# A hybrid decoder layer on one core: decode values as the stationary operand, the merge weighted by VectorE, and the third pattern's query blocks two at a time

## The chip, the core and the metric

The kernel runs on one core of a Trainium2 chip. The metric is the device time of one execution in microseconds (us), lower is better. The engines work side by side, each in the order in which its instructions stand: TensorE (PE, its weight loads PEld), VectorE (DVE), ScalarE (ACT), GpSimd (POOL), and SyncE (SP), which issues nearly all transfers and so holds one ordered queue of DMA issues.

## The reference, cut to what matters

One layer for a prompt of 1024 positions and eight decode sequences of one token. A single projection gives q, k and v for three attention patterns (8 heads of 64, dilation 1, 4 and 16) and the inputs of a Mamba-2 branch. Each pattern gives an output and a softmax sum per position; the three are merged by those sums; the merged 512 columns and 1024 columns of the gated, normalised Mamba branch go through one output projection.

```python
for g, (window, dil) in enumerate(ATTN_PATTERNS):
    o, lse = dilated_window_prompt(q, k, v, dil)      # prompt; softmax over at most 129 keys
    outs.append(o); lses.append(lse)
attn = merge_patterns(outs, lses)                     # softmax over the three patterns, weighted sum
...
sc = jnp.einsum('bthd,btkhd->bthk', q, sel_k) * ATTN_SCALE          # decode: 128 cached keys and the new one
o = jnp.einsum('bthk,btkhd->bthd', softmax(sc), sel_v)
...
mix = jnp.concatenate([attn, ssm], axis=-1) @ w_out
```

## The kernel before, in words

All activations lie transposed, 128 features by 1032 positions (1024 of the prompt and 8 decode tokens), eight such tiles for 1024 features. A projection of 128 output columns is called a gemm here: three chunks of 344 positions, each of 24 matmuls (L176: eight k tiles, three products of a high and a low part). Its weights are loaded to `wr` (L149), rounded to `wh` by ScalarE (L164), and the rest `wl` is made by VectorE (L165); the second matmul of a chunk needs `wl`.

The code is written in stages, but the order on each engine is set when the program is built, by a list scheduler with priorities ("evac", "w", "side", "late", "main") and its own estimates of time; small work is thus put between the matmuls of long gemms. At run time each engine keeps that order and waits on semaphores.

The stage that the change touches runs from about 780 to 1040 us. In it stand, one inside the other:

- **Pattern 2** (`attend`, L633): for each of four head pairs and eight blocks of 128 queries, score matmuls (L649), VectorE adds the mask and takes the maximum in one instruction with an accumulator (L655) and scales it (L659), ScalarE takes the exponential with a sum (L663), PE transposes (L670), a copy (L674 or L676), PE multiplies with the values (L683). The result goes to DRAM (`n_d`).
- **The z gemms** 0 to 7, 72 matmuls each; VectorE multiplies each into `yg[k]` (L886).
- **The merge** (L818 to L862, priority "late"): from the softmax sums the weights `wo` are made on VectorE (L844), transposed on PE (L845), stored to `w_d` and loaded back spread over partitions as `wt`. Then 16 merges, one for each 256 positions and head pair: load `nt` (three patterns, 384 KB) and `wt`, multiply (L858, GpSimd), two adds (L859, L860, VectorE), round to `ah` (L861, ScalarE), `al` = rest (L862, VectorE). `nt` and `wt` have two buffers each, so the load of merge k+2 waits for L862 of merge k.
- **Decode values** (L895 to L925): 24 loads `cvt` (eight sequences, three patterns, 128 cached rows of 512) on six buffers, 24 multiplies by the probabilities `dpt` (16 on GpSimd, 8 on VectorE), 16 adds on VectorE (L910, L911), eight matmuls with a selecting column (L912), four transposes.
- **The SSM output projection**: after the last z gemm ScalarE and VectorE make `sh` and `sl` of `yg` (L935, L936), and the first two column blocks are multiplied (L957), k tile by k tile; the rest are gemms again.

Of the kernel before, what the change touches and what calls it, by code (L numbers as in the profile page):

```python
# [50 lines left out]
def trunk(tc, a, o):  # L51
# [581 lines left out]
    def attend(g, hp, qr, kr, vt):  # L633
# [58 lines left out]
                                   nps.rearrange("p (r i) -> p r i", i=S // d))  # L692
        nc.sync.dma_start(out=n_d[g, hp], in_=nh)

    def pattern(g):
        for hp in range(HP):
            vt = do_v(g, hp)
            qr = do_qk(g, hp, 0)
            kr = do_qk(g, hp, 1)
            with prio("side"):  # L700
                attend(g, hp, qr, kr, vt)
        with prio("side"):
            stt = ac.tile([P, 8, 16], F32, name=f"stt{g}")
# [114 lines left out]
    with prio("late"):  # L818
# [30 lines left out]
        for q in range(S // QT):  # L849
            for hp in range(HP):  # L850
                qs = slice(q * QT, (q + 1) * QT)
                nt = mgp.tile([P, NG, QT], F32, tag="nt", name="nt")
                nc.sync.dma_start(out=nt, in_=n_d[:, hp, :, qs].rearrange("g p t -> p g t"))
                wt = mgp.tile([P, NG, QT], F32, tag="wt", name="wt")
                for h in range(2):
                    nc.sync.dma_start(out=wt[h * 64:(h + 1) * 64],
                                      in_=w_d[:, 2 * hp + h, qs].unsqueeze(0).to_broadcast([64, NG, QT]))
                nc.gpsimd.tensor_tensor(out=nt, in0=nt, in1=wt, op=ALU.mult)  # L858
                nc.vector.tensor_tensor(out=nt[:, 0], in0=nt[:, 0], in1=nt[:, 1], op=ALU.add)  # L859
                nc.vector.tensor_tensor(out=nt[:, 0], in0=nt[:, 0], in1=nt[:, 2], op=ALU.add)  # L860
                nc.scalar.copy(ah[:, hp, qs], nt[:, 0])  # L861
                nc.vector.tensor_tensor(out=al[:, hp, qs], in0=nt[:, 0], in1=ah[:, hp, qs], op=ALU.subtract)  # L862
# [30 lines left out]
                    nc.gpsimd.tensor_tensor(out=acc, in0=acc, in1=zt, op=ALU.add)  # L893

    with prio("late"):  # L895
        sel = cap.tile([P, NB * NB], F32, name="sel")
        nc.vector.memset(sel, 0.0)
        nc.vector.memset(sel[:, 0:NB * NB:NB + 1], 1.0)
        ops = att_ps("nps")
        for b in range(NB):  # L900
            vts = []
            for g in range(NG):
                vt = cvp.tile([P, 512], F32, tag="cv", name="cvt")
                nc.sync.dma_start(out=vt, in_=a[f"cache{g}"][b].rearrange("(k r) c -> r k c", r=DIL[g])[0, :, 512:1024])
                pw = dpt[:, g].rearrange("p h (x b) -> p b x h", b=NB)[:, b].unsqueeze(3)
                v4 = vt.rearrange("p (x h d) -> p x h d", x=HP, h=2)
                (nc.gpsimd if g else nc.vector).tensor_tensor(out=v4, in0=v4, in1=pw.to_broadcast([P, HP, 2, 64]),
                                                              op=ALU.mult)
                vts.append(vt)
            nc.vector.tensor_tensor(out=vts[0], in0=vts[0], in1=vts[1], op=ALU.add)  # L910
            nc.vector.tensor_tensor(out=vts[0], in0=vts[0], in1=vts[2], op=ALU.add)  # L911
            behind(nc.tensor.matmul(ops[:NB], sel[:, b * NB:(b + 1) * NB], vts[0], start=(b == 0), stop=(b == NB - 1)),  # L912
                   zlast[CACHE[b]])
        osb = cvp.tile([NB, 512], F32, tag="cv", name="osb")
        nc.scalar.copy(osb, ops[:NB])
        otp = att_ps("nps")
        for hp in range(HP):
            nc.tensor.transpose(otp[:, hp * NB:(hp + 1) * NB], osb[:, hp * P:(hp + 1) * P], ident[:NB, :NB])
        nc.vector.tensor_tensor(out=dat, in0=otp[:, 0:HP * NB], in1=dnv[:, 0], op=ALU.add)
        for g in range(1, NG):  # L920
            nc.vector.tensor_tensor(out=dat, in0=dat, in1=dnv[:, g], op=ALU.add)
        dv = dat.rearrange("p (h b) -> p h b", h=HP)
        nc.scalar.copy(ah[:, :, S:T], dv)
        nc.vector.tensor_tensor(out=al[:, :, S:T], in0=dv, in1=ah[:, :, S:T], op=ALU.subtract)
# [582 lines left out]
```

## Time and profile before

| what | value |
|---|---|
| time, median of 3 runs | 1864.06 us (1863.29 to 1867.74) |
| the profiled execution | 1859.84 us, its span 1858.1 us |
| PE busy in the span | 1773.7 us (95%) |
| VectorE, ScalarE, GpSimd busy | 1143.8, 782.1, 320.4 us |
| mean granted clock of TensorE | 0.982 |

PE is the bound nearly everywhere, so what counts is the time in which it waits or runs at half clock. A timeline row gives start, duration, engine, line, operation, tiles, and in brackets how long the engine had been idle and what ended that. A busy PE row is a model of a pipelined matmul; the distance between two starts tells more than the duration.

### The profile page before, as it was taken

What the parts mean: (1) busy time and instruction counts of PE and PEld (TensorE: products, weight loads), DVE (VectorE), ACT (ScalarE), POOL (GpSimd) and SP (SyncE); (2) the same over time, 40 slices, a digit from 0 to 9 for tenths busy, and PEclk for the clock granted to TensorE, in tenths of its full rate; (3) what the DMA queues carried; (4) which work ended last, traced back from release to release, by engine and by line L of the source; (5) the groups of instructions that cost most, each with busy time, mean ns of one, the idle gap of its engine ahead of it and who ended that gap; (6) DMA issues with size and microseconds to landing.
All of it is one profiled execution on the core that took longest, in us unless ns stands there. A gap on an engine that the chain in (4) does not pass through costs nothing.

```text
span 1858.1 us, 30703 instructions
## 1 busy us (share of the span) xinstructions
PE 1773.7 (95%) x12189; PEld 1659.7 (89%) x12189; DVE 1143.8 (62%) x2236; ACT 782.1 (42%) x1441; POOL 320.4 (17%) x217
## 2 busy tenths in 40 slices
PE   8999999999998999999879999999999999999995
PEld 6999877888887888988768999999999999999995
DVE  6545666776765454446577599886666666423338
ACT  5533554465544555556343335532222222431133
POOL 0000244544224221123342300000000000000020
PEclk9999999999999999999989999999999999999998
DMA  4322344434334243346566345364454445876686
GB/s 156 136 99 79 96 127 124 130 121 125 105 103 156 90 141 108 117 158 230 154 172 187 108 155 178 111 211 166 172 175 159 177 152 204 335 276 205 207 316 206
DMA packets 135200, 298.61 MB, mean 161 GB/s; under 512 B 18432, under 2 KB 85600, under 8 KB 133648
## 3 DMA queue, kind: packets, MB, share of 16 engines
q1 hardware_dynamic: 135056, 296.64, 48.2%
q8 instruction: 96, 1.57, 0.4%
q14 instruction: 48, 0.39, 0.1%
HBM read 247.49 MB, written 137.10 MB: 207 GB/s over the span
## 4 chain that ended last, share of the span: by engine, by line
PE 37%; DVE 8%; DMA 4%; issue 1%; ACT 1%; POOL 0%; SPq 0%; DVEq 0%; POOLq 0%; ACTq 0%
PE fb L1230 21%; PE g L176 15%; DMA nt<-n_d 2%; PE pg L176 1%; PE pu L176 1%; DVE wl L165 1%; DVE xr L1056 1%; DVE sl L936 1%; DVE nacc L1013 1%; DMA hr<-hid_d 0%; DMA cvt<-in_cache 0%; DVE nt L859 0%; POOL nt L858 0%; DMA wr<-in_w_fin 0%; DVE fl L1071 0%
## 5 line engine op out<-in xcount | busy, mean ns | idle before, releaser
L176 PE MATMUL g<-xh,wh 128*128 128x344 f32 x1344 | 445.0, 331 | 4.4 <-ACT rw L589 3.7
L176 PE MATMUL g<-xh,wl 128*128 128x344 f32 x1344 | 438.9, 327 | 7.2 <-DVE wl L165 7.2
L176 PE MATMUL g<-xl,wh 128*128 128x344 f32 x1344 | 440.6, 328 | 1.5 <-DVE xl L234 1.5
L176 PEld LDWEIGHTS g<-xh,wh 128*128 128x128 f32 x1344 | 256.5, 191 | 17.8 <-issue 8.4
L176 PEld LDWEIGHTS g<-xh,wl 128*128 128x128 f32 x1344 | 257.0, 191 | 15.0 <-DVE wl L165 8.0
L176 PEld LDWEIGHTS g<-xl,wh 128*128 128x128 f32 x1344 | 256.9, 191 | 7.8 <-issue 4.9
L1230 PE MATMUL fb<-fh,wsl 128*128 128x258 f32 x1216 | 222.3, 282 | 0.0
L1230 PEld LDWEIGHTS fb<-fh,wsl 128*128 128x128 f32 x1216 | 187.9, 189 | 0.0
L1230 PE MATMUL fb<-fl,wsl 128*128 128x258 f32 x608 | 171.7, 283 | 0.0
L165 DVE TENSOR_TENSOR wl<-wr,wh 128x1024 fp32r<-128x1024 f32 (+1 forms) x93 | 113.6, 1222 | 82.5 <-ACT wh L164 82.3
L176 PE MATMUL g<-hh,wh 128*128 128x344 f32 x432 | 137.9, 319 | 0.8 <-ACT fac L1297 0.8
L176 PE MATMUL g<-hh,wl 128*128 128x344 f32 x432 | 137.7, 319 | 0.0
L176 PE MATMUL g<-hl,wh 128*128 128x344 f32 x432 | 136.7, 320 | 0.0
L164 ACT CAST wh<-wr 128x1024 fp32r<-128x1024 f32 (+1 forms) x93 | 92.4, 995 | 93.5 <-PE g L176 87.8
L663 ACT ACTIVATE sm<-sm,ngm 128x128 f32<-128x128 f32 (+1 forms) x192 | 84.8, 443 | 108.9 <-DVE ngm L659 103.9
L1313 POOL TENSOR_TENSOR ow<-wr,ow 128x512 fp32r<-128x512 f32 x8 | 10.9, 1395 | 659.6 <-ACT ow L1312 659.6
L619 POOL TENSOR_TENSOR sw<-sw,sin 128x1032 f32<-128x1032 f32 x24 | 73.4, 3059 | 250.6 <-ACT sw L618 187.1
L1230 PEld LDWEIGHTS fb<-fl,wsl 128*128 128x128 f32 x608 | 114.8, 189 | 0.0
L618 ACT COPY sw<-rw 32x1032 f32<-32x1032 f32 x96 | 101.0, 1052 | 1.4
L589 ACT COPY rw<-g 128x344 f32<-128x344 f32 x108 | 47.2, 442 | 112.1 <-PE g L176 70.4
L1234 DVE TENSOR_TENSOR fo<-fp,fb 128x258 f32<-128x258 f32 x152 | 62.8, 420 | 46.1 <-PE fb L1230 43.7
L176 PEld LDWEIGHTS g<-hh,wh 128*128 128x128 f32 x432 | 81.1, 188 | 1.1 <-ACT fac L1297 1.1
(362 smaller groups left out, 3789.8 us busy)
## 6 DMA issues: line engine op xcount, KB each, us to landing
out_skv<-in_cache SPq DMA_DIRECT2D x64, 1023.5 KB, 5.8
wr<-in_w_in SPq DMA_DIRECT2D x56, 512.0 KB, 3.7
out_skv<-in_cache SPq DMA_DIRECT2D x16, 1022.0 KB, 5.5
wr<-in_w_out SPq DMA_DIRECT2D x24, 512.0 KB, 3.7
hr<-hid_d SPq DMA_DIRECT2D x22, 516.0 KB, 6.2
hid_d<-fo SPq DMA_DIRECT2D x38, 258.0 KB, 4.2
wg<-in_w_fin SPq DMA_DIRECT2D x19, 512.0 KB, 4.6
wu<-in_w_fin SPq DMA_DIRECT2D x19, 512.0 KB, 5.0
```

The costliest lines, as they stand in the source:

```text
L164: nc.scalar.copy(wh[:, :cols], wr[:, :cols])
L165: nc.vector.tensor_tensor(out=wl[:, :cols], in0=wr[:, :cols], in1=wh[:, :cols], op=ALU.subtract)
L176: last = nc.tensor.matmul(ps, x[:, ws], y[:, c0:c1], start=(k == 0 and j == 0), stop=(k == n - 1 and j == 2))
L589: return nc.scalar.copy(rw[:, c0:c1], ps)
L618: nc.scalar.copy(sw[q * 32:(q + 1) * 32, 0:T], rw[s * 32:(s + 1) * 32, :])
L619: nc.gpsimd.tensor_tensor(out=sw[:, 0:T], in0=sw[:, 0:T], in1=sin, op=ALU.mult)
L663: nc.scalar.activation(out=sm[:, h, :nk], in_=sm[:, h, :nk], func=AF.Exp, scale=SCALE, bias=ngm[:, g, j, i:i + 1], accum_out=den[:, g, j, ...
L936: nc.vector.scalar_tensor_tensor(out=lo, in0=yg[k][:, cs_], scalar=nw(SSD_NORM, k), in1=hi, op0=ALU.mult, op1=ALU.subtract)
L1013: nc.vector.tensor_tensor(out=acc, in0=acc, in1=sq, op=ALU.add)
L1056: nc.vector.scalar_tensor_tensor(out=h, in0=mv, scalar=nw(MIX_POST, m), in1=h, op0=ALU.mult, op1=ALU.add)
L1230: nc.tensor.matmul(ps, x[:, ks], y, start=(k == 0 and j == 0), stop=(k == 3 and j == 2))
L1234: return nc.vector.tensor_tensor(out=dst, in0=x, in1=y, op=ALU.add)
```

## The change

Three edits. (1) Pattern 2 goes through a new function `attend2`: two query blocks at a time, the mask added by two 128x256 instructions, one maximum, one subtraction and one sum over 128x512 on VectorE, one exponential of 128x512 on ScalarE. The matmuls are the same in number, in bursts of four. (2) The merge multiply goes from GpSimd to VectorE. (3) The decode values become the stationary operand: 96 products (each two instructions in the trace, as the float32 matmuls of before are) of a 128x128 block of `cvt` with the two probability columns of its heads replace the multiplies, the adds, the selecting matmuls and the transposes; the `cvt` buffers are freed by PE. No pool is changed.

```diff
+    def attend2(hp, qr, kr, vt):
...
+        for j in range(0, 8, 2):
+            sps = [att_ps("sps") for _ in range(2)]
...
+            for h in range(2):
+                nc.vector.tensor_tensor(out=sm[:, h], in0=sps[h][:, 0:2 * P].rearrange("p (i k) -> p i k", i=2),
+                                        in1=mask2.unsqueeze(1).to_broadcast([P, 2, P]), op=ALU.add)
+            i2 = slice(hp * 2, hp * 2 + 2)
+            mv = mx[:, g, j:j + 2, i2].rearrange("p i h -> p h i")
+            nc.vector.tensor_reduce(out=mv, in_=sm, op=ALU.max, axis=AX.X)
+            nc.vector.tensor_tensor(out=sm, in0=sm, in1=mv.unsqueeze(3).to_broadcast([P, 2, 2, P]), op=ALU.subtract)
+            nc.scalar.activation(out=sm, in_=sm, func=AF.Exp, scale=SCALE)
+            nc.vector.tensor_reduce(out=den[:, g, j:j + 2, i2].rearrange("p i h -> p h i"), in_=sm, op=ALU.add,
+                                    axis=AX.X)
+            tp = att_ps("ptp")
+            for h in range(2):
+                for i in range(2):
+                    q = h * 2 + i
+                    nc.tensor.transpose(tp[:, q * P:(q + 1) * P], sm[:, h, i], ident)
...
-                nc.gpsimd.tensor_tensor(out=nt, in0=nt, in1=wt, op=ALU.mult)
+                nc.vector.tensor_tensor(out=nt, in0=nt, in1=wt, op=ALU.mult)
...
-                pw = dpt[:, g].rearrange("p h (x b) -> p b x h", b=NB)[:, b].unsqueeze(3)
-                v4 = vt.rearrange("p (x h d) -> p x h d", x=HP, h=2)
-                (nc.gpsimd if g else nc.vector).tensor_tensor(out=v4, in0=v4, in1=pw.to_broadcast([P, HP, 2, 64]),
-                                                              op=ALU.mult)
                 vts.append(vt)
-            nc.vector.tensor_tensor(out=vts[0], in0=vts[0], in1=vts[1], op=ALU.add)
-            nc.vector.tensor_tensor(out=vts[0], in0=vts[0], in1=vts[2], op=ALU.add)
-            behind(nc.tensor.matmul(ops[:NB], sel[:, b * NB:(b + 1) * NB], vts[0], start=(b == 0), stop=(b == NB - 1)),
-                   zlast[CACHE[b]])
...
+            for x in range(HP):
+                q = x * NB + b
+                for g in range(NG):
+                    ins = nc.tensor.matmul(ops[:, 0:64].rearrange("p (h c) -> p h c", h=2)[:, :, q],
+                                           vts[g][:, x * P:(x + 1) * P], dpt[:, g, :, q], start=(g == 0),
+                                           stop=(g == NG - 1))
+                    if x == 0 and g == 0:
+                        behind(ins, zlast[CACHE[b]])
```

The scheduler then puts everything in another order. On VectorE before, the end of the z gemms reads as follows (L859, L860 and L862 belong to a merge, whose multiply is on GpSimd; L936 makes `sl` for the first SSM matmuls; six merges stand ahead of this first `sl`, the seventh between the first and the second):

```order
L886 TENSOR_TENSOR yg_9266<-yg_9266,zt 128x1032
L860 TENSOR_TENSOR nt<-nt 128x256
L859 TENSOR_TENSOR nt<-nt 128x256
L860 TENSOR_TENSOR nt<-nt 128x256
L862 TENSOR_TENSOR al<-nt,ah 128x256 x2
L936 SCALAR_TENSOR_TENSOR sl_9476<-yg_8721,par,sh_9475 128x688
L936 SCALAR_TENSOR_TENSOR sl_9476<-yg_8721,par,sh_9475 128x344
L859 TENSOR_TENSOR nt<-nt 128x256
L936 SCALAR_TENSOR_TENSOR sl_9478<-yg_8811,par,sh_9477 128x688
L936 SCALAR_TENSOR_TENSOR sl_9478<-yg_8811,par,sh_9477 128x344
L860 TENSOR_TENSOR nt<-nt 128x256
L936 SCALAR_TENSOR_TENSOR sl_9480<-yg_8902,par,sh_9479 128x688
```

After the change (L909 is the merge multiply, L910, L911 and L913 are L859, L860 and L862 of before, L982 is L936) the same place reads:

```order
L910 TENSOR_TENSOR nt<-nt 128x256
L911 TENSOR_TENSOR nt<-nt 128x256
L982 SCALAR_TENSOR_TENSOR sl_9387<-yg_8593,par,sh_9386 128x688
L982 SCALAR_TENSOR_TENSOR sl_9387<-yg_8593,par,sh_9386 128x344
L982 SCALAR_TENSOR_TENSOR sl_9389<-yg_8683,par,sh_9388 128x688
L982 SCALAR_TENSOR_TENSOR sl_9389<-yg_8683,par,sh_9388 128x344
L909 TENSOR_TENSOR nt<-nt,wt 128x768
L913 TENSOR_TENSOR al<-nt,ah 128x256
L982 SCALAR_TENSOR_TENSOR sl_9391<-yg_8774,par,sh_9390 128x688
L982 SCALAR_TENSOR_TENSOR sl_9391<-yg_8774,par,sh_9390 128x344
L910 TENSOR_TENSOR nt<-nt 128x256
L165 TENSOR_TENSOR wl<-wr,wh 128x1024
```

The merge multiplies are now on this engine, and fifteen of the sixteen merges stand ahead of the first `sl`. The weights' rest `wl` for the second SSM block (L165) stands behind the sixteenth.

On SP's queue before, around the store of the merge weights (L848), the loads of `nt` (L853), `wt` (L856), `cvt` (L904) and weights (L149) stand so:

```order
L853 DMA nt<-n_d 128x3x256 x2
L904 DMA cvt<-in_cache 128x512 x2
L848 DMA w_d<-wts 64x3x128
L856 DMA wt<-w_d 64x3x256 x4
L904 DMA cvt<-in_cache 128x512 x2
L856 DMA wt<-w_d 64x3x256 x2
L904 DMA cvt<-in_cache 128x512
L856 DMA wt<-w_d 64x3x256 x2
L904 DMA cvt<-in_cache 128x512
L149 DMA wr<-in_w_out 128x1024
L853 DMA nt<-n_d 128x3x256
L904 DMA cvt<-in_cache 128x512 x2
```

After (L899 is L848, L904 is the load of `nt`, L907 of `wt`, L952 of `cvt`):

```order
L904 DMA nt<-n_d 128x3x256 x2
L149 DMA wr<-in_w_in 128x1024
L899 DMA w_d<-wts 64x3x128
L907 DMA wt<-w_d 64x3x256 x4
L952 DMA cvt<-in_cache 128x512
L907 DMA wt<-w_d 64x3x256 x4
L904 DMA nt<-n_d 128x3x256
L952 DMA cvt<-in_cache 128x512
L904 DMA nt<-n_d 128x3x256
L952 DMA cvt<-in_cache 128x512 x4
L907 DMA wt<-w_d 64x3x256 x3
L904 DMA nt<-n_d 128x3x256
```

The `cvt` loads of the rest of the third and of the fourth sequence (three for each) now stand behind the loads of the third and fourth `nt`, which wait for the first two merges. On PE, the transposes of the merge weights stand 25 L176 matmuls earlier than before (after 3803 from the start, not 3828), the 96 products of decode values stand in bursts of 24, 24, 12, 12, 12 and 12 between the z gemms, and 229 L176 matmuls lie between those transposes and the first SSM matmul. Pattern 2's work, 57 bursts between the matmuls of the gemms before, stands in 34.

## Rows read from the trace of the kernel before

**Rows 1.** The page: busy us, share of the span, instructions of each engine.

```profile
PE 1773.7 (95%) x12189; PEld 1659.7 (89%) x12189; DVE 1143.8 (62%) x2236; ACT 782.1 (42%) x1441; POOL 320.4 (17%) x217
```

**Rows 2.** Waits of PE, 894 to 1045 us: engine, line, releaser, us, times, longest.

```profile
PE g L176 <- DVE wl L165: 11.5, 6, 4.1
...
PE g L957 <- DVE sl L936: 5.2, 1, 5.2
```

**Rows 3.** Timeline of PE: start, us, operation, [idle before it, what ended that].

```profile
899.79 0.66 PE L176 MATMUL g<-xh,wl 128*128 128x344 f32 x1 [4.09 <-DVE wl L165]
...
900.53 0.49 PE L176 MATMUL g<-xh,wh 128*128 128x344 f32 x1
...
905.70 0.36 PE L176 MATMUL g<-xh,wh 128*128 128x344 f32 x1
...
929.42 0.47 PE L176 MATMUL g<-xh,wl 128*128 128x344 f32 x1 [2.58 <-DVE wl L165]
```

**Rows 4.** Timeline of VectorE, 895 to 900 us.

```profile
897.91 0.69 DVE L911 TENSOR_TENSOR cvt<-cvt 128x512 f32<-128x512 f32 x1 [2.02 <-POOL cvt L907]
...
898.52 1.22 DVE L165 TENSOR_TENSOR wl<-wr,wh 128x1024 fp32r<-128x1024 f32 x1
```

**Rows 5.** Timeline of VectorE, 921 to 975 us.

```profile
924.17 1.99 DVE L860 TENSOR_TENSOR nt<-nt 128x256 f32<-128x256 f32 x1
...
960.22 0.42 DVE L859 TENSOR_TENSOR nt<-nt 128x256 f32<-128x256 f32 x1 [2.57 <-POOL nt L858]
...
962.75 1.42 DVE L936 SCALAR_TENSOR_TENSOR sl<-yg,par,sh 128x688 fp32r<-128x688 f32 x2 [0.69 <-ACT sh L935]
```

**Rows 6.** Timeline of PE at the first SSM matmuls.

```profile
971.04 0.65 PE L957 MATMUL g<-sl,wh 128*128 128x344 f32 x1 [5.25 <-DVE sl L936]
```

**Rows 7.** Timeline of PE around one attention burst.

```profile
879.68 0.32 PE L176 MATMUL g<-xh,wh 128*128 128x344 f32 x1
...
879.93 0.44 PE L683 MATMUL nps<-pt,vt 128*64 128x128 f32 x4
...
880.73 0.32 PE L176 MATMUL g<-xl,wh 128*128 128x344 f32 x1
...
880.89 0.32 PE L176 MATMUL g<-xh,wh 128*128 128x344 f32 x1
```

**Rows 8.** Groups by line and shape: count, busy us, mean ns, idle before.

```profile
L165 DVE TENSOR_TENSOR wl<-wr,wh 128x768 fp32r<-128x768 f32 x24 | 23.0, 957 | 29.8 <-ACT wh L164 29.8
...
L474 DVE TENSOR_REDUCE yd<-tm 128x4 f32<-128x512 f32 x16 | 11.0, 685 | 20.1 <-POOL tm L473 20.1
...
L663 ACT ACTIVATE sm<-sm,ngm 128x256 f32<-128x256 f32 x88 | 43.9, 500 | 48.4 <-DVE ngm L659 48.1
```

**Rows 9.** Timeline of PE, 905 to 913 us.

```profile
911.98 0.38 PE L845 MATMUL wtp<-ident,wo 128*64 128x128 f32 x2
```

**Rows 10.** Timeline of GpSimd, 905 to 990 us.

```profile
921.86 1.82 POOL L858 TENSOR_TENSOR nt<-nt,wt 128x768 f32<-128x768 f32 x1 [10.63 <-DMA wt<-w_d]
...
936.89 2.28 POOL L858 TENSOR_TENSOR nt<-nt,wt 128x768 f32<-128x768 f32 x1
...
981.62 1.98 POOL L858 TENSOR_TENSOR nt<-nt,wt 128x768 f32<-128x768 f32 x1 [11.77 <-DMA nt<-n_d]
```

**Rows 11.** DMA issues, 900 to 1030 us: count, KB each, median us to landing.

```profile
nt<-n_d SPq DMA_DIRECT2D x16, 384.0 KB, 4.9
```

**Rows 12.** Timeline of the DMA queue of SP, 912 to 985 us.

```profile
929.82 0.38 SPq L853 DMA_DIRECT2D nt<-n_d  x1
...
977.88 2.13 SPq L853 DMA_DIRECT2D nt<-n_d  x2
```

**Rows 13.** Windows: us, busy (instructions) of five engines, granted clock, DMA share, GB/s.

```profile
930.00:940.00 10.00, 10.00 (x51) 8.93 (x51) 8.73 (x8) 4.17 (x6) 6.51 (x4) 0.85 0.90 280
```

**Rows 14.** Timeline of PE: eight small matmuls; four of 128 columns.

```profile
198.41 0.66 PE L440 MATMUL dtp<-ident,dex 8*128 8x8 f32 x8
...
242.01 0.66 PE L670 MATMUL ptp<-ident,sm 128*128 128x128 f32 x4
```

More of the change, by code (lines that the diff above doesn't have):

```diff
@@ L693, in attend @@
         nc.sync.dma_start(out=n_d[g, hp], in_=nh)
+    def attend2(hp, qr, kr, vt):
+        g = 2
+        nh = nhp.tile([P, S], F32, tag="nh", name="nh")
+        for j in range(0, 8, 2):
+            sps = [att_ps("sps") for _ in range(2)]
+            for jj in (j, j + 1):
+                for h in range(2):
+                    hs = slice(h * 64, (h + 1) * 64)
+                    c0 = (jj % 2) * P
+                    js = slice(jj * P, (jj + 1) * P)
+                    nc.tensor.matmul(sps[h][:, c0:c0 + P], qr[hs, js], kr[hs, js], start=True, stop=True)
+            sm = smp.tile([P, 2, 2, P], F32, tag="sm", name="sm")
+            for h in range(2):
[9 more added lines that the diff above has]
+            tp = att_ps("ptp")
+            for h in range(2):
+                for i in range(2):
+                    q = h * 2 + i
+                    nc.tensor.transpose(tp[:, q * P:(q + 1) * P], sm[:, h, i], ident)
+            pt = ptp.tile([P, 4, P], F32, tag="pt", name="pt")
+            dst = pt.rearrange("p q t -> p (q t)")
+            if j % 4:
+                nc.scalar.copy(dst, tp)
+            else:
+                nc.vector.tensor_copy(dst, tp)
+            if j % 4 == 0:
+                nps = att_ps("nps")
+            for i in range(2):
+                for h in range(2):
+                    hs = slice(h * 64, (h + 1) * 64)
+                    nc.tensor.matmul(nps[hs, (j % 4 + i) * P:(j % 4 + i + 1) * P], vt[:, j + i, hs], pt[:, h * 2 + i],
+                                     start=True, stop=True)
+            if j % 4 == 2:
+                d = DIL[g]
+                rr = slice((j - 2) * d // 8, (j + 2) * d // 8)
+                nc.scalar.copy(nh.rearrange("p (i r) -> p r i", r=d)[:, rr],
+                               nps.rearrange("p (r i) -> p r i", i=S // d))
+        nc.sync.dma_start(out=n_d[g, hp], in_=nh)
@@ L700, in pattern @@
             with prio("side"):
-                attend(g, hp, qr, kr, vt)
+                if g == 2:
+                    attend2(hp, qr, kr, vt)
+                else:
+                    attend(g, hp, qr, kr, vt)
         with prio("side"):
@@ L895, in trunk @@
     with prio("late"):
-        sel = cap.tile([P, NB * NB], F32, name="sel")
-        nc.vector.memset(sel, 0.0)
-        nc.vector.memset(sel[:, 0:NB * NB:NB + 1], 1.0)
         ops = att_ps("nps")
@@ L904, in trunk @@
                 nc.sync.dma_start(out=vt, in_=a[f"cache{g}"][b].rearrange("(k r) c -> r k c", r=DIL[g])[0, :, 512:1024])
-                pw = dpt[:, g].rearrange("p h (x b) -> p b x h", b=NB)[:, b].unsqueeze(3)
-                v4 = vt.rearrange("p (x h d) -> p x h d", x=HP, h=2)
-                (nc.gpsimd if g else nc.vector).tensor_tensor(out=v4, in0=v4, in1=pw.to_broadcast([P, HP, 2, 64]),
-                                                              op=ALU.mult)
                 vts.append(vt)
-            nc.vector.tensor_tensor(out=vts[0], in0=vts[0], in1=vts[1], op=ALU.add)
-            nc.vector.tensor_tensor(out=vts[0], in0=vts[0], in1=vts[2], op=ALU.add)
-            behind(nc.tensor.matmul(ops[:NB], sel[:, b * NB:(b + 1) * NB], vts[0], start=(b == 0), stop=(b == NB - 1)),
-                   zlast[CACHE[b]])
[L914 to L919, printed above, removed]
+            for x in range(HP):
[6 more added lines that the diff above has]
+                        behind(ins, zlast[CACHE[b]])
+        for h in range(2):
+            hs = slice(h * 64, (h + 1) * 64)
+            nc.vector.tensor_tensor(out=dat[hs], in0=ops[hs, h * 32:(h + 1) * 32], in1=dnv[hs, 0], op=ALU.add)
         for g in range(1, NG):
```

## The prediction

> **What bounds the kernel now.** I read the page first: PE is busy in 1773.7 of 1858.1 us [rows 1], so an edit elsewhere counts only where PE waits or is slowed. The waits of PE in 894 to 1045 us, the stretch with the end of pattern 2, the merge and the decode values, come next [rows 2]: 11.5 us in six waits for `wl` and 5.2 us in one for `sl`, both made by VectorE. The timeline says what lies ahead of them. The longest, 4.09 us, ends at 899.79 [rows 3]; VectorE made that `wl` at 898.52, behind L911, which had waited for a multiply of decode values on GpSimd [rows 4]. After such a stall PE is also slow: from 900.53 to 905.70 [rows 3] eighteen matmuls start 0.29 us apart, where 0.16 us is the pace elsewhere (880.73 to 880.89 [rows 7]), so it ran at the lower of its two clock levels, 1.2 GHz, after the idle time. The last one, 5.25 us at 971.04 [rows 6], waits for the second `sl`, which stands behind the seventh merge. So the merge chain paces this stretch, and it is paced by itself: two buffers, and a load of `nt` that must wait for L862 two merges before.
>
> **Terms, edit by edit.** *Decode values.* The multiplies on GpSimd that held up `wl` are gone: the stall of 4.1 us at 899.79 goes, and with it the slow matmuls, 18 and three ahead of them, 0.13 us each, 2.7 us. In their place PE gets 96 products, 192 instructions. The trace has no such product. Bounds: eight small matmuls take 0.66 us, 0.083 us for one; four of 128 columns also take 0.66, 0.165 us for one [rows 14]. So 15.8 to 31.7 us; they move only two columns, so I take the lower value, 16 us. The Trainium skill (TensorE: Matmul & The Clock Gate, section LDWEIGHTS) would have a load of 128 columns take 107 ns, for which I estimate 20.5 us for 192; rows 14 show less for one small matmul, and no row shows 192 in a line. None of this is on the path if PE waits for the merge chain anyway, which the next sums decide.
>
> *Pattern 2.* A burst between two gemm matmuls costs about 0.09 us at its start: 879.68 to 879.93 is 0.25 us where 0.16 is the pace [rows 7]; I take the same at its end. Twenty-three bursts fewer (57 to 34), 0.18 us each, save 4.1 us. The softmax of one step becomes longer: two mask adds of 0.42 (960.22 has the size [rows 5]), a maximum and a subtraction of 0.69, an exponential that I put at 0.71 (0.50 us for 256 columns [rows 8], and twice that as an upper end). With hand-offs of 0.5 us that is 3.4 us from scores to transposes; the nearest stand 27 gemm matmuls apart, 4.2 us. It is covered, by 0.8 us. Uncovered it would cost up to 0.8 us in each of 16 steps.
>
> *The merge.* Its start comes earlier. The transposes of the weights end PE's part at 911.98 [rows 9]. From that go 4.1 and 2.7 (the stall and its slow matmuls), 4.1 (pattern 2) and 25 matmuls by which they stand earlier, 3.9 us: 897.2. The first multiply started 9.9 us behind them (921.86 [rows 10]), so 907.1 now. Of each merge, the multiply falls from 1.82 us or more [rows 10] to 0.96 (the 128x768 subtraction of VectorE [rows 8]); the two adds are 0.42 each when GpSimd is quiet (960.22), where one of them took 1.99 us at 924.17 while GpSimd multiplied [rows 5]. That contention goes away with the multiplies. The Trainium skill (SBUF — State Buffer, section SBUF: two separate sides) calls the port pair of the two engines an exclusive lock; by that rule the adds come back to 0.42, and the trace agrees.
>
> But 15 merges now stand ahead of the first `sl`, where six did. From one L862 to that of the merge two later: landing of `nt`, 4.9 us as the median [rows 11], then 0.96, two adds of 0.42, `ah` with hand-offs 0.53 and `al` 0.42, 2.75 in all; the other buffer's merge runs in the time of the landing. A leg is 7.65 us. The first L862 ends about 4 us behind the first multiply; then come seven legs, 53.6 us, and in three of them a `wl` and a `yg`, both near 1.22 us (898.52 is a `wl` [rows 4]), 7.3 us. The first `sl` starts at 907.1 + 4.0 + 53.6 + 7.3 = 972.0. It takes 0.92 us of the 1.42 of the two [rows 5], and PE then has six matmuls, 1.4 us at a pace between the two, up to the point that it reached at 971.04. That is 974.3, **3.3 us later**.
>
> Is PE there in time? From the transposes it has 229 gemm matmuls, 36 us, 16 us of products, and waits for `cvt` and `wl`. The `cvt` of the third sequence are issued behind the fourth `nt`, so behind the second L862, about 4.5 us after the first multiply; with a landing of 4.9 and the queue's issues they are there some 20 us behind the transposes, where PE asks for them at 13.9 (61 gemm matmuls and 26 products): 6 us. 897.2 + 36 + 16 + 6 = 955. PE waits for `sl` some 17 us, so neither the products nor the `cvt` waits count; at 31.7 us for the products the two arrive together.
>
> *Behind it.* After the first `sl` only one merge is left. Of the 11.5 us of waits for `wl`, 4.1 are counted and 2.6 were the one at 929.42 [rows 3]; it may stay, hidden. The other 4.8 us lie behind 990, where merges of before stood between `wl` and the mix and where SP's queue held weights behind `wt`. They go. The second block's `wl` stands behind the sixteenth merge, and three pairs of `sl` rows: 2.8 + 0.96 + 0.42 + 1.4 + 0.42 + 1.22 = 7.3 us behind the start of the first `sl`, where PE needs it after 0.92 and 34 matmuls of 0.16, 6.2: 1.1 us back.
>
> **The sum.** +3.3 - 4.8 + 1.1 = -0.4 us on the profiled 1859.84, so 1859.4. That execution is 4.2 us under the median of the runs, 1864.06, so the forecast is 1863.7 on that scale. No change: what the start of the merge gains (14.8 us) the longer chain ahead of `sl` takes. Less than 0.3%, 5.6 us, the measurement of this kernel cannot tell from no change.
>
> **Range.** One number decides: the landing, which counts seven times. Issue to multiply took 3.74 us at best (977.88 to 981.62) and 7.07 with two other loads ahead (929.82 to 936.89) [rows 10, 12]. That is -8.1 or +15.2 us: 1855.6 to 1878.9. The start is uncertain by some 4 us (pattern 2), so 1848 to 1882.
>
> **Rivals.**
> 1. *The loads pace the chain: slower.* In 930 to 940 us the DMA engines were 0.90 busy at 280 GB/s [rows 13], and a leg moves two merges (1.5 MB), three `cvt` (0.77) and part of a weight: 2.6 MB, at 280 GB/s 9.3 us, more than 7.65. With 7.07 us a landing the time is 1879. It decides from a landing of 5.8 us on, where the sum passes 5.6 us. For it: the nearest loaded stretch is just this one. Against: the first legs alone hold the `cvt` loads.
> 2. *The loads come quickly: faster.* Where only merges load, 3.74 us a landing; with a start 4 us earlier besides it is 1863.7 - 8.1 - 4 = 1851.6. For it: GpSimd and its locks are gone. Against: the first legs have more loads beside them than any of before.
> 3. *Pattern 2 takes its gain back.* The longer softmax runs into VectorE's `wl` and `yg` rows: 0.8 us in 16 steps, 12.8 us, and the start of the merge moves with it: 1876. For it: the cover is 0.8 us, and one add of VectorE held up by 1.5 us, as at 924.17, breaks it. Against: the order has 27 matmuls only where it is tightest, up to 39 elsewhere.
> 4. *PE's products become the bound.* At 0.165 us each PE arrives with `sl`, no change; with two slow stretches like that behind 899.79 besides, 5.4 us: 1869.
>
> **Chances.** The forecast 0.37, the first rival 0.20, the second 0.31, the third and fourth 0.12 together. Faster by over 0.3%: 0.31. Within 0.3%: 0.38. Slower: 0.31. The range holds all but the ends of the first rival and of the second with more than one wait gone.
>
> **What would show it.** Right: no wait for `wl` near 899; the transposes of the merge weights at about 897; GpSimd with five adds in the stretch; VectorE's 128x256 adds at 0.42 all through; 15 multiplies by 972, about 7.65 to 9 us from pair to pair; one wait of PE of over 10 us for the first `sl` at L1003, ended near 973; products in bursts with waits for `cvt` ahead of the third; no wait for `wl` in 1000 to 1045 but the second block's. Wrong: a first `sl` before 962 or after 982; no long wait for it, PE arriving last; waits of PE for transposes in 790 to 890 us, one a step.

## The result, and the profile after

The change is slower. The median is 1875.26 us (1873.70 to 1876.88, 4 runs) against 1864.59 us of the kernel before (4 runs); the ratio is 1.0066, 95% interval 1.0046 to 1.0087. The forecast was 1863.7 us, no change that can be measured. The profiled execution took 1876.54 us with a span of 1874.8, 16.7 us more than the span of before.

The page of the kernel after, its row of busy time and the granted clock in 40 slices (before: [rows 1]):

```profile
PE 1789.7 (95%) x12361; PEld 1689.1 (90%) x12361; DVE 1136.4 (61%) x2131; ACT 766.6 (41%) x1328; POOL 270.3 (14%) x185
...
PEclk9999999999999999999888999999999999999998
```

PE is busy 16.0 us longer than before, with 172 instructions more, and the clock row has three slices of 8 in a row in the middle. Its idle time in the span is nearly the same, 85.1 us and 84.4 before. So the net loss is in the work and the pace of PE; its waits have changed their places. The waits of PE from 894 to 1045 us in the kernel after (before: [rows 2]):

```profile
PE g L1003 <- ACT sh L981: 9.4, 1, 9.4
...
PE nps L958 <- DMA cvt<-in_cache: 7.4, 6, 3.0
...
PE g L176 <- DVE wl L165: 0.3, 1, 0.3
```

The waits for `wl`, 11.5 us before, are down to 0.3. One wait of 9.4 us stands at the first SSM matmuls, and 7.4 us go to loads of `cvt`. Where they lie, in the timeline of PE after:

```profile
900.49 0.53 PE L896 MATMUL wtp<-ident,wo 128*64 128x128 f32 x3 [1.89 <-issue]
...
988.86 0.94 PE L1003 MATMUL g<-sh,wh 128*128 128x344 f32 x2 [9.40 <-ACT sh L981]
```

The transposes of the merge weights stand at 900.49 (911.98 before [rows 9], 897.2 forecast). The stall at 899.79 [rows 3] is gone. PE came to the first SSM matmul (L1003) at 988.86 - 9.40 = 979.5 and then waited; before it was there at 962.77 - 1.74 = 961.0, and it resumed for good at 971.04 [rows 6]:

```profile
962.77 0.58 PE L957 MATMUL g<-sh,wh 128*128 128x344 f32 x2 [1.74 <-ACT sh L935]
```

PE itself comes 18.5 us later than before, though its transposes stand 11.5 us earlier: it takes 79.0 us from them to this point, where it took 49.0. The merges, in the timeline of VectorE after (L909 multiply, L913 `al`, L982 `sl`). The rows are the chain of one buffer, merges 1, 3, 5 to 15; the other buffer's stand between, and where L913 has x2 it is the first of the two in the row of 914.08 and the second in the others:

```profile
909.43 0.96 DVE L909 TENSOR_TENSOR nt<-nt,wt 128x768 f32<-128x768 f32 x1 [8.77 <-DMA wt<-w_d]
...
914.08 0.98 DVE L913 TENSOR_TENSOR al<-nt,ah 128x256 fp32r<-128x256 f32 x2
919.96 0.96 DVE L909 TENSOR_TENSOR nt<-nt,wt 128x768 f32<-128x768 f32 x1 [4.90 <-DMA nt<-n_d]
...
923.06 0.42 DVE L913 TENSOR_TENSOR al<-nt,ah 128x256 fp32r<-128x256 f32 x1
...
930.77 0.96 DVE L909 TENSOR_TENSOR nt<-nt,wt 128x768 f32<-128x768 f32 x1 [3.87 <-DMA nt<-n_d]
...
933.11 0.43 DVE L913 TENSOR_TENSOR al<-nt,ah 128x256 fp32r<-128x256 f32 x1 [0.47 <-ACT ah L912]
...
940.47 0.96 DVE L909 TENSOR_TENSOR nt<-nt,wt 128x768 f32<-128x768 f32 x1 [2.69 <-DMA nt<-n_d]
...
942.82 0.42 DVE L913 TENSOR_TENSOR al<-nt,ah 128x256 fp32r<-128x256 f32 x1 [0.47 <-ACT ah L912]
...
951.14 0.95 DVE L909 TENSOR_TENSOR nt<-nt,wt 128x768 f32<-128x768 f32 x1
...
955.25 0.97 DVE L913 TENSOR_TENSOR al<-nt,ah 128x256 fp32r<-128x256 f32 x2
...
964.49 0.95 DVE L909 TENSOR_TENSOR nt<-nt,wt 128x768 f32<-128x768 f32 x1
...
966.49 0.98 DVE L913 TENSOR_TENSOR al<-nt,ah 128x256 fp32r<-128x256 f32 x2
...
975.04 0.95 DVE L909 TENSOR_TENSOR nt<-nt,wt 128x768 f32<-128x768 f32 x1
...
980.37 0.43 DVE L913 TENSOR_TENSOR al<-nt,ah 128x256 fp32r<-128x256 f32 x1 [0.75 <-ACT ah L912]
...
987.18 0.95 DVE L909 TENSOR_TENSOR nt<-nt,wt 128x768 f32<-128x768 f32 x1
...
989.17 0.93 DVE L982 SCALAR_TENSOR_TENSOR sl<-yg,par,sh 128x688 fp32r<-128x688 f32 x1
```

The first multiply is at 909.43 (forecast 907.1), the fifteenth at 987.18, so seven pairs take 77.8 us, 11.1 each. The first `sl` starts at 989.17 (forecast 972.0). A load of `nt` is issued when L913 of the merge two before has ended (0.5 us behind it at most). From that end to the multiply are 5.5, 7.3, 6.9, 7.9, 8.3, 7.6 and 6.4 us, 49.8 in all, 7.1 each. The rest of the chain, 22.9 us in six merges and 2.0 in the fifteenth, is the time from a multiply to the end of its L913, with the `wl` and `yg` that stand between. Merges 5 and 7 take 2.8 us from the multiply to the end of L913, each alone; from the tenth merge on the two buffers run in phase (963.16 and 964.49, 973.71 and 975.04, 985.38 and 987.18), so that the second multiply stands 1.3 to 1.8 us behind the first.

PE's wait ends on `sh`, not `sl`, because ScalarE too has merges ahead of it; its timeline after (L912 `ah`):

```profile
987.29 0.41 ACT L912 CAST ah<-nt 128x256 fp32r<-128x256 f32 x1 [6.96 <-DVE nt L911]
```

ScalarE was idle for 6.96 us, waiting for the adds of the fourteenth merge, while the `sh` that PE needed (L981, at 987.94) stood behind.

### The profile page after: what moved, and what is told of

The parts are those of the page before. It is cut to its first block, busy times and chain, and to the rows that moved or that the text cites. A ratio compares the mean times of both kernels' runs of the same rounds, so it can differ in the third digit from the quotient of the medians.

```text
span 1874.8 us, 30733 instructions
## 1 busy us (share of the span) xinstructions
PE 1789.7 (95%) x12361; PEld 1689.1 (90%) x12361; DVE 1136.4 (61%) x2131; ACT 766.6 (41%) x1328; POOL 270.3 (14%) x185
## 4 chain that ended last, share of the span: by engine, by line
PE 44%; DVE 5%; DMA 4%; issue 1%; ACT 1%; POOL 0%; SPq 0%; DVEq 0%; POOLq 0%; ACTq 0%
PE fb L1276 20%; PE g L176 19%; DMA nt<-n_d 3%; PE pg L176 2%; PE pu L176 2%; DMA qb<-qd_d 1%; DVE nt L909 1%; DVE nacc L1059 0%; PE g L1003 0%; DVE mix L1114 0%; DVE fac L1400 0%; DMA wt<-w_d 0%; DVE nt L911 0%; DMA out_yT<-fac 0%; DVE wl L165 0%
## 5 line engine op out<-in xcount | busy, mean ns | idle before, releaser
L176 PE MATMUL g<-xh,wh 128*128 128x344 f32 x1344 | 445.5, 332 | 4.3 <-ACT rw L589 3.6
L176 PE MATMUL g<-xl,wh 128*128 128x344 f32 x1344 | 441.3, 329 | 1.5 <-DVE xl L234 1.5
L176 PE MATMUL g<-xh,wl 128*128 128x344 f32 x1344 | 439.5, 327 | 0.5 <-DVE wl L165 0.5
L176 PEld LDWEIGHTS g<-xh,wh 128*128 128x128 f32 x1344 | 257.4, 192 | 13.6 <-ACT rw L589 6.2
L176 PEld LDWEIGHTS g<-xh,wl 128*128 128x128 f32 x1344 | 257.7, 192 | 8.3 <-issue 6.3
L176 PEld LDWEIGHTS g<-xl,wh 128*128 128x128 f32 x1344 | 257.6, 192 | 7.7 <-issue 5.1
L165 DVE TENSOR_TENSOR wl<-wr,wh 128x1024 fp32r<-128x1024 f32 (+1 forms) x93 | 110.9, 1194 | 90.2 <-ACT wh L164 90.0
L176 PE MATMUL g<-hh,wh 128*128 128x344 f32 x432 | 137.9, 319 | 0.1
L176 PE MATMUL g<-hh,wl 128*128 128x344 f32 x432 | 137.6, 319 | 0.0
L176 PE MATMUL g<-hl,wh 128*128 128x344 f32 x432 | 136.8, 320 | 0.0
L1359 POOL TENSOR_TENSOR ow<-wr,ow 128x512 fp32r<-128x512 f32 x8 | 10.9, 1389 | 657.8 <-ACT ow L1358 657.8
L663 ACT ACTIVATE sm<-sm,ngm 128x256 f32<-128x256 f32 (+1 forms) x128 | 59.7, 468 | 82.1 <-DVE ngm L659 81.6
L176 PEld LDWEIGHTS g<-hh,wh 128*128 128x128 f32 x432 | 81.1, 188 | 0.3 <-ACT fac L1343 0.3
```

The costliest lines, as they stand in the source:

```text
L165: nc.vector.tensor_tensor(out=wl[:, :cols], in0=wr[:, :cols], in1=wh[:, :cols], op=ALU.subtract)
L176: last = nc.tensor.matmul(ps, x[:, ws], y[:, c0:c1], start=(k == 0 and j == 0), stop=(k == n - 1 and j == 2))
L663: nc.scalar.activation(out=sm[:, h, :nk], in_=sm[:, h, :nk], func=AF.Exp, scale=SCALE, bias=ngm[:, g, j, i:i + 1], accum_out=den[:, g, j, ...
L1359: nc.gpsimd.tensor_tensor(out=wl, in0=src, in1=wh, op=ALU.subtract)
```

## The experiments

Each was timed beside the kernel before; ratios are to it, with 95% intervals. The change itself has 1.0066.

**Fewer merges ahead of `sl`.** The merges became a function; the first eight stay where they were, the others come behind the `sl` loop, behind one of its instructions:

```diff
+        for i in range(8):
+            merge(i // HP, i % HP)
...
+                if (k, cs_.start) == (3, 0):
+                    gate = lo_ins
...
+    with prio("late"):
+        for i in range(8, 16):
+            merge(i // HP, i % HP, gate)
+    rst.close()
```

> The change with merges 9 to 16 emitted behind the first sl instructions, so that 8 merges stand ahead of the first sl on VectorE where the change has 15; nothing else differs. Theory A (the merge chain ahead of the first sl, about 10.4 us for two merges, sets the end of the stretch; PE's products and their cvt waits are hidden): all that was lost comes back, about 1858 to 1862 us. Theory B (PE's own work from the transposes of the merge weights to the first SSM matmul, 79 us in the trace of the change, is nearly as late as the chain): only the 9.4 us of PE's last wait can come back, about 1866 us, and PE's wait for sh or sl is then under 2 us.

Measured: 1855.74 us, ratio 0.9959 (0.9941 to 0.9977), 0.4% faster than before and, by the ratios, 1.1% faster than the change, some 20 us. VectorE's first `sl` and PE's first SSM matmul, in its timelines:

```profile
968.85 3.61 DVE L984 SCALAR_TENSOR_TENSOR sl<-yg,par,sh 128x688 fp32r<-128x688 f32 x5 [7.69 <-PE g L176]
...
973.76 0.56 PE L1011 MATMUL g<-sh,wh 128*128 128x344 f32 x2
```

PE no longer waits there; it arrives itself at 973.76, 5.7 us sooner than in the change. Theory A had 1858 to 1862; the run is 2 us below that, so all of the loss came back and a little more. Theory B's limit of 9.4 us falls: PE also comes sooner (its transposes by 1.8 us, its waits for `cvt` 5.5 us for 7.4), and the granted clock is 1.00 in 970 to 990 us, where the change, behind its long wait, has 0.50 in 980 to 990. By the two profiled executions 21.0 us come back: the wait of 9.4, the 5.7, and 5.9 behind this point, which these rows do not explain in full.

**And half of the products.** As above, and for three of the four column blocks only the first pattern's product; half of the decode values' sum is left out.

```diff
-                for g in range(NG):
+                gs = range(NG) if x == 0 else range(1)
+                for g in gs:
                     ins = nc.tensor.matmul(ops[:, 0:64].rearrange("p (h c) -> p h c", h=2)[:, :, q],
```

> As the kernel with 8 merges ahead of the first sl, and with half of the products of decode values left out (for three of the four column blocks only the first pattern's product is made; all 24 loads stay, each cvt tile is still read once). 8 merges ahead in both. Theory A: the same time as with all products, within 3 us. Theory B: PE arrives at the first SSM matmul 12 to 15 us earlier than with all products and the time falls by 8 us or more against that kernel, to about 1855 us.

Measured: 1845.84 us, ratio 0.9919 (0.9891 to 0.9947), 0.4% under the run with all products, some 7 to 10 us. PE's first SSM matmul, its products from 890 to 985 us, and a window (us, busy of PE, PEld, DVE, ACT, POOL, clock, DMA share, GB/s):

```profile
952.50 0.56 PE L1012 MATMUL g<-sh,wh 128*128 128x344 f32 x2
```

```profile
L962 PE MATMUL nps<-dpt,cvt 128*128 128x2 f32 x96 | 11.8, 243 | 0.7 <-DMA cvt<-in_cache 0.6
```

```profile
930.00:940.00 10.00, 10.00 (x70) 10.00 (x68) 5.37 (x8) 3.05 (x7) 2.41 (x1) 1.00 1.06 321
```

With half the products PE arrives 21 us sooner (952.50 for 973.76), more than theory B asked for. Between the transposes and this point 14 us of it are the products, 5 are waits for `cvt`, and 3 are gemm matmuls that no longer run at the lower clock level. The two profiled executions are 12.9 us apart, so some 8 us are given back behind this point; no row here shows where. So once the merges are out of the way PE's own work, the products first, is the limit. Theory A, by which they are hidden, falls for this order. The products of the kernel after, for comparison, and two windows of it:

```profile
L958 PE MATMUL nps<-dpt,cvt 128*128 128x2 f32 x192 | 27.2, 271 | 7.5 <-DMA cvt<-in_cache 7.4
```

```profile
930.00:940.00 10.00, 9.95 (x52) 9.86 (x53) 4.47 (x8) 1.15 (x3) 0.16 (x1) 0.67 1.07 276
...
950.00:960.00 10.00, 9.76 (x67) 9.65 (x67) 6.05 (x8) 2.58 (x5) 2.58 (x1) 1.00 0.85 221
```

96 instructions take 11.8 us, 192 take 27.2, 0.14 us each. With half of them the clock is 1.00 in 930 to 940 us; in the change it is 0.67 there, though PE is busy 9.95 of the 10 us. In the run with all products and the same merges ahead it is 0.84.

**The change without each edit.** Decode values as before, the other two edits kept (against the change):

```diff
+                (nc.gpsimd if g else nc.vector).tensor_tensor(out=v4, in0=v4, in1=pw.to_broadcast([P, HP, 2, 64]),
+                                                              op=ALU.mult)
...
-                    ins = nc.tensor.matmul(ops[:, 0:64].rearrange("p (h c) -> p h c", h=2)[:, :, q],
-                                           vts[g][:, x * P:(x + 1) * P], dpt[:, g, :, q], start=(g == 0),
```

> The change without the edit on decode values: multiplies, adds and selecting matmuls as before; merge multiply on VectorE, third pattern two blocks at a time. The order has 8 merges ahead of the first sl. Theory A: near the kernel before or faster, 1858 to 1864 us, because of the 8 merges. Theory B: the same number for another reason (no products, PE runs the stretch in some 55 us). This run tells the edit that costs, not the reason: if it is still above 1870, both are wrong and the merge multiply or the third pattern costs.

Measured: 1848.95 us, ratio 0.9935 (0.9910 to 0.9959): with that edit undone the change is 0.65% faster than before, and 0.2% faster than with the edit and the same eight merges ahead (0.9959; the two intervals overlap). By these ratios most of what the edit costs is the seven merges, and the products themselves cost less. PE at the first SSM matmuls, in an execution that took 1855.70 us, the longest of four (the others 1847.3 to 1849.0):

```profile
966.77 0.94 PE L1008 MATMUL g<-sl,wh 128*128 128x344 f32 x2 [6.17 <-DVE sl L987]
```

PE resumes at 966.77, 4.3 us sooner than before [rows 6]. The old third pattern, the other two edits kept:

```diff
-                if g == 2:
-                    attend2(hp, qr, kr, vt)
-                else:
-                    attend(g, hp, qr, kr, vt)
+                attend(g, hp, qr, kr, vt)
```

> The change without the new third pattern; merge multiply on VectorE and decode values as stationary operand stay; 15 merges ahead of the first sl, as in the change. Theories A and B: as slow as the change, plus the 4 us that the bursts of the third pattern save: 1875 to 1880 us. If it is below 1868, the third pattern's edit is the cost, which neither theory has.

Measured: 1880.86 us, ratio 1.0098 (1.0081 to 1.0115), 0.3% above the change (the intervals just overlap), with a wait of 12.46 us at the same place:

```profile
987.72 0.94 PE L952 MATMUL g<-sh,wh 128*128 128x344 f32 x2 [12.46 <-ACT sh L930]
```

The merge multiply back on GpSimd, the other two edits kept; 13 merges ahead of `sl`:

```diff
-                nc.vector.tensor_tensor(out=nt, in0=nt, in1=wt, op=ALU.mult)
+                nc.gpsimd.tensor_tensor(out=nt, in0=nt, in1=wt, op=ALU.mult)
```

> The change with the merge multiply back on GpSimd; 13 merges ahead of the first sl for 15. One pair fewer is 11 us less, six pairs with 1.8 us more of multiplies are 11 us more: 1870 to 1880 us, so the merge multiply's place does not make the loss. Below 1866 it would.

Measured: 1878.07 us, ratio 1.0081 (1.0057 to 1.0105), as expected. PE's second wait at the first SSM matmuls:

```profile
985.07 0.94 PE L1003 MATMUL g<-sl,wh 128*128 128x344 f32 x2 [9.39 <-DVE sl L982]
```

**Each edit alone**, against the kernel before. First the decode values:

```diff
+                    ins = nc.tensor.matmul(ops[:, 0:64].rearrange("p (h c) -> p h c", h=2)[:, :, q],
+                                           vts[g][:, x * P:(x + 1) * P], dpt[:, g, :, q], start=(g == 0),
```

> The kernel before with the decode values' edit alone; the merge multiply stays on GpSimd, and the order has 15 merges ahead of the first sl. Theory (what costs is the order that this edit brings about, by which the scheduler lets 15 merges pass): as slow as the change or slower, 1876 to 1886 us, since the multiply is 0.9 us longer. If the loss needs the multiply on VectorE, it is near the kernel before, under 1868 us.

Measured: 1883.41 us, ratio 1.0103 (1.0078 to 1.0128). The edit on decode values alone makes all of the loss and more. Its trace has 13 merges ahead of the first `sl`, not the 15 of the expectation:

```profile
994.69 0.94 PE L952 MATMUL g<-sh,wh 128*128 128x344 f32 x2 [10.22 <-ACT sh L930]
```

The third pattern alone:

```diff
+                if g == 2:
+                    attend2(hp, qr, kr, vt)
```

> The kernel before with the third pattern's edit alone. The prediction's term (23 bursts fewer, 4.1 us): 0.2% below the kernel before. If the longer softmax took it back (third rival), no gain or slower. The run without this edit was 5.6 us slower than the change, which speaks for 4 to 6 us.

Measured: 1866.68 us, ratio 1.0017 (1.0005 to 1.0028): no gain, a little slower, against the prediction's term and on the side of its third rival. Its waits from 894 to 1045 us:

```profile
PE nps L963 <- DVE cvt L962: 7.0, 2, 5.6
...
PE g L1008 <- DVE sl L987: 6.9, 1, 6.9
```

In the order that this edit leads to, PE waits for the decode values' multiplies and the merges in other places; between 780 and 895 us PE's waits come to 3.2 us in all, so the third rival's mechanism, a wait in each step of the third pattern, is not there.

The merge multiply alone:

```diff
-                nc.gpsimd.tensor_tensor(out=nt, in0=nt, in1=wt, op=ALU.mult)
+                nc.vector.tensor_tensor(out=nt, in0=nt, in1=wt, op=ALU.mult)
```

> The kernel before with the merge multiply on VectorE alone; 6 merges stand ahead of the first sl, as before. The multiply falls from 1.85 to 0.96 us and VectorE is no longer held up by it, but GpSimd still multiplies decode values: 4 to 8 us faster than before (0.2 to 0.4%). If the merge chain is paced by its loads alone, no more than 2 us.

Measured: 1862.64 us, ratio 1.0000 (0.9987 to 1.0012): no change, where 4 to 8 us were expected. The waits for `wl` are 10.4 us, nearly as before; GpSimd still multiplies decode values, behind which the longest of them stood before [rows 4]:

```profile
PE g L176 <- DVE wl L165: 10.4, 4, 4.1
```

**What makes a pair slow.** Leaving out 21 of the 24 loads of `cvt` and using three tiles for all eight sequences:

```diff
+        vts = []
         for b in range(NB):
-            vts = []
             for g in range(NG):
+                if b:
+                    break
                 vt = cvp.tile([P, 512], F32, tag="cv", name="cvt")
```

> The change with 21 of the 24 loads of decode values left out: the three cvt tiles of the first sequence are used for all eight (so the decode values are those of one sequence), with all 96 products as before. The order has 16 merges ahead of the first sl. Theory D (the landing of nt is long, 6.8 us in the change, because cvt loads stand beside it in the queue): the landing falls to 5 us or less, a pair of merges takes 8 us or less, the first sl starts near 975 and the time is 1858 to 1866 us. Theory E (the pair itself makes it long: both nt and four wt, 1.5 MB, go into the queue together once the two buffers run in phase): the landing stays over 6 us, the first sl stays near 989 and the time is 1871 to 1877 us.

Measured: 1870.84 us, ratio 1.0039 (1.0026 to 1.0053). The first and fifteenth multiply, the landing of `nt` from 895 to 1000 us, PE's wait for `wl`, and PE at the first SSM matmul:

```profile
906.64 0.96 DVE L909 TENSOR_TENSOR nt<-nt,wt 128x768 f32<-128x768 f32 x1 [9.31 <-DMA wt<-w_d]
...
982.82 0.96 DVE L909 TENSOR_TENSOR nt<-nt,wt 128x768 f32<-128x768 f32 x1 [2.38 <-DMA nt<-n_d]
```

```profile
nt<-n_d SPq DMA_DIRECT2D x14, 384.0 KB, 5.7
```

```profile
PE g L176 <- DVE wl L165: 9.3, 1, 9.3
```

```profile
988.70 0.94 PE L1005 MATMUL g<-sh,wh 128*128 128x344 f32 x2 [15.53 <-ACT sh L983]
```

Seven pairs take 76.2 us, 10.9 each, nearly as in the change, and PE, now free of `cvt` waits, stands 9.3 us for a `wl` that VectorE makes behind the multiplies of merges 9 and 10, and then 15.53 us. The landing fell from a median of 6.8 us in the change (897 to 1000 us) to 5.7:

```profile
nt<-n_d SPq DMA_DIRECT2D x14, 384.0 KB, 6.8
```

So without the `cvt` loads the landing is 1.1 us shorter. Neither theory has its condition, 5 us or less for D and over 6 for E; the place of the first `sl` (988.7) is that of theory E. In the chain of merges 1, 3, 5 to 15 the seven waits for a load come to 43.2 us where the change has 49.8, but VectorE's part is longer by more than that: sixteen merges stand ahead, all pairs run in phase, and two of the merges' rows took 2.4 and 2.5 us beside an add of GpSimd. The run therefore does not tell what a shorter landing alone is worth.

A third `nt` buffer (and five `cvt` buffers for six):

```diff
-                nt = mgp.tile([P, NG, QT], F32, tag="nt", name="nt")
+                nt = mgp.tile([P, NG, QT], F32, tag="nt", name="nt", bufs=3)
```

> The change with three nt buffers where it has two (and five cvt buffers for six, to fit): the load of a merge then no longer waits for the L862 of the merge two before. All 16 merges stand ahead of the first sl. Theory E (the round trip of the loads behind two buffers that run in phase paces the chain, 10.8 us for a pair): a pair takes 8 us or less, the first sl starts near 965 to 972, PE's last wait shrinks and the time is 1860 to 1868 us. Theory F (the bandwidth of the loads paces it): a pair still takes 10 us or more and the time is 1874 us or more.

Measured: 1870.58 us, ratio 1.0037 (1.0021 to 1.0053), between the two theories. First and fifteenth multiply, PE's arrival, its waits from 880 to 1045 us, and a window:

```profile
900.22 0.96 DVE L909 TENSOR_TENSOR nt<-nt,wt 128x768 f32<-128x768 f32 x1 [9.07 <-DMA wt<-w_d]
...
968.74 0.96 DVE L909 TENSOR_TENSOR nt<-nt,wt 128x768 f32<-128x768 f32 x1 [1.47 <-DMA wt<-w_d]
```

```profile
985.84 0.92 PE L1003 MATMUL g<-sh,wh 128*128 128x344 f32 x2
```

```profile
PE nps L958 <- DMA cvt<-in_cache: 15.8, 9, 4.6
```

```profile
960.00:970.00 10.00, 7.33 (x44) 7.33 (x45) 5.04 (x9) 3.06 (x5) 0.00 (x0) 0.83 1.11 235
```

A pair takes 9.8 us, between theory E's 8 and theory F's 10. The wait for a buffer was only part: the landing rises to a median of 7.8 us, the DMA engines' share is 1.11 (1.07 in 930 to 940 us of the change, and 1.09 in the 10 us behind; the share can pass 1), and PE loses 15.8 us to loads of `cvt` that stand in the same queue, so that it arrives last, at 985.84, five microseconds behind `sl`.

**Looking for more.** The kernel without the edit on decode values, with 6 merges ahead of `sl` (the function of the first experiment):

```diff
+        for i in range(6):
+            merge(i // HP, i % HP)
```

> The kernel without the stationary operand (merge multiply on VectorE and third pattern two blocks at a time, decode values as before), with merges 7 to 16 emitted behind the first sl instructions: 6 merges ahead of the first sl where it had 8. If the place of sl among the merges sets the wait of 6.2 us for sl in that kernel, the wait goes and the time falls by 4 to 6 us, from 1849 to 1843 to 1845 us. If the wait only moves (to wl behind the later merges) the time stays within 2 us of 1849.

Measured: 1850.09 us, ratio 0.9926 (0.9910 to 0.9941), the same as with 8. Its waits:

```profile
PE g L176 <- DVE wl L165: 8.7, 5, 4.0
...
PE g L1016 <- ACT sh L988: 0.4, 2, 0.2
```

The wait at the first SSM matmuls is gone (0.4 us), the waits for `wl` stay (8.0 us with 8 merges), and the time does not fall. The trace with 8 merges is of the longest execution of its four, so no row shows where the 6 us went. With a third `nt` buffer besides:

```diff
-    cvp = pool(rst, "cvp", 6, side="right")
+    cvp = pool(rst, "cvp", 5, side="right")
```

> The faster kernel (merge multiply on VectorE, third pattern two blocks at a time, decode values as before, merges 7 to 16 behind the first sl) with three nt buffers and five cvt buffers. If the waits for wl that are left (8 to 10 us in six) come from merges late by the round trip, they halve: 1844 to 1847 us. If they come from the weights' own loads: within 2 us of 1850.

Measured: 1857.91 us, ratio 0.9971 (0.9959 to 0.9984): slower, so neither expectation holds. PE's waits for `wl` from 894 to 1045 us did halve, to 3.8 us, as the first one said. In their place PE waits 6.8 us for the decode values' adds, 3.8 for the transposes of the merge weights and 3.8 for the mix. The order changed with the buffers, and which of its moves costs is open.

## Why the prediction was wrong

The chain of merges ahead of the first `sl` was named by the prediction, and its first rival, the same chain with a landing of 7.07 us, 1879 us and a chance of 0.20, is what came. (The third rival's 1876 is nearer as a number, by luck: its waits are not there.) The step that failed is one term of the sum, the landing of 4.9 us in "a leg is 7.65 us", which counts seven times. Measured are 7.1 us from the end of L913 to the multiply two merges later: 49.8 us for seven, where the sum had 34.3. VectorE's part of the chain was sized well, 24.9 us where the sum had 26.6 (seven times 2.75, and 7.3 for `wl` and `yg`). Together it gave 60.9 us from the first L862 to the first `sl`, and 74.7 are measured; the first multiply was 2.3 us late and the first merge 1.1 us longer. The 4.9 us were the median of before, where fewer loads stood together; in the change the DMA engines' share is 1.07 in 930 to 940 us, where it was 0.90 [rows 13]. "The other buffer's merge runs in the time of the landing" holds for merges 5 and 7; where the buffers run in phase, 1.3 to 1.8 us of a wait is the other merge. That the DMA engines make the landing long is the likely reading, not shown by one run alone: without the `cvt` loads it was still 5.7 us, and with a third buffer 7.8.

The second step that failed is PE's own arrival: forecast 955, measured 979.5. "16 us of products" took 27.2 us, within the bounds of 15.8 to 31.7 but near the upper, and their price is higher than that. Of the 229 gemm matmuls between the transposes and PE's arrival, 60 ran 0.29 us apart, where 0.16 is the pace: the granted clock fell to the lower of its two levels, 1.2 GHz. The first burst of products and the gemm matmuls behind it, in the timeline of PE after, and a window of it (columns as above):

```profile
904.62 6.33 PE L958 MATMUL nps<-dpt,cvt 128*128 128x2 f32 x48
...
911.24 0.49 PE L176 MATMUL g<-xh,wl 128*128 128x344 f32 x1
...
915.25 0.49 PE L176 MATMUL g<-xh,wh 128*128 128x344 f32 x1
```

```profile
909.00:915.60 6.60, 6.60 (x27) 6.60 (x27) 4.20 (x8) 0.81 (x2) 0.00 (x0) 0.50 0.68 172
```

The clock is 1.00 in 904.6 to 908.8 us and falls inside the burst, at 908.9; 14 matmuls from 911.24 to 915.25 take 4.0 us. PE had been idle for 1.89 us in front of its transposes, 8 us before. That this idle time is not the cause shows in the run with the decode values' edit alone: there PE was not idle between 885 us and its first burst, and the clock fell in the burst all the same:

```profile
910.79 6.89 PE L907 MATMUL nps<-dpt,cvt 128*128 128x2 f32 x48
```

```profile
914.60:921.20 6.60, 6.60 (x28) 6.60 (x29) 3.09 (x5) 0.40 (x1) 3.62 (x2) 0.50 0.84 200
```

Not every burst is followed by it: in the change the one of 24 at 948.92 was not (the clock is 1.00 in 950 to 960 us). From the transposes to PE's arrival were 79 us, where the prediction had 58: 11 us more of products, 1.4 more of waits for `cvt`, and the rest, some 8 us, gemm matmuls at the lower level. The Trainium skill (TensorE: Matmul & The Clock Gate, section LDWEIGHTS) gives 107 ns for a load of 128 columns, an estimate of 20.5 us for 192; the trace has 0.14 us each over all, 0.11 at the full clock (the first 40 of the first burst) and 0.21 at the lower level, so the page's figure fits the full clock and was nearer than the row that I took. A half of the products, with fewer merges, saves 7 to 10 us: measured, not argued.

By its other steps. *The stall at 899.79* went, as said, with the multiplies on GpSimd; what is left on that engine from 860 to 1045 us are the five adds and little else:

```profile
L944 POOL TENSOR_TENSOR acc<-acc,zt 128x1032 f32<-128x1032 f32 x5 | 12.3, 2469 | 81.3 <-ACT zt L942 81.3
```

*The contention* went too where GpSimd is idle: the adds take 0.42 us; one, at 952.79, took 2.53 us beside an add of GpSimd of 2.58 us (952.47). *The third pattern* as -4.1 us is not settled: beside the other two edits it is worth 0.3%, alone it costs 0.17%, and each of the two runs has its own order. The transposes stand 11.5 us earlier instead of 14.8; 1.89 us of that is idle time of PE right in front of them. *Behind it*: between the point where PE resumes (971.04 before; the second `sl` at 992.04 after, 21.0 us later) and the end (16.7 us later) 4.3 us come back, 3.7 were predicted. *No wait for PE's arrival*: PE was 9.4 us ahead of `sh`, not 17.

So in the change PE stands 9.4 us for the chain of merges, where it stood 1.7 and 5.2 us at the same matmuls before, and its own way there is 18.5 us later than before. Taking seven merges out of the way gives back more than the 9.4, some 20 us, because PE comes sooner too and restarts at the full clock. What is not settled: why the third pattern and the merge multiply, each without gain alone, give 0.65% together. Each run has another order, and no run holds the order fixed.

## What to carry to other kernels

A load time that counts many times in a sum wants its own check: a median landing taken from a stretch with fewer loads in the queue was too short by 2 us, seven times over, and the forecast fell with it. Before adding buffers look at the DMA engines' share: here it was about 1, and a third buffer moved the wait to another tile's loads. An edit on one engine can change the order on all: here 15 merges passed ahead of the first `sl` where 6 had stood. (Why the scheduler did so, its estimates of PE's time perhaps, is not shown.) So count what stands ahead of the first urgent instruction, then gate it by hand. Many small matmuls between long ones can cost more than their own time: here 60 of 229 long ones ran at half pace behind the bursts, so time the stretch, not the burst.

## What the runs showed that I had not expected

In a burst of 48 product instructions the granted clock fell, and some 16 gemm matmuls behind it ran at 0.29 us; it was 0.67 in 930 to 940 us with PE busy 9.95 us of 10. A third buffer for the loads raised their landing from 6.8 to 7.8 us and moved the wait to the loads of another tile. Edits with no gain alone (ratios 1.0017 and 1.0000) gave 0.9935 together.
